# A hybrid decoder step whose free engines get their order from the scheduler's timeline model instead of its core model

## The chip, the cores and the metric

The kernel runs on one core of one Trainium2 chip. What is measured is the time of one execution on the device, in microseconds (us). TensorE (PE in the profile; PEld is its weight load), VectorE (DVE), ScalarE (ACT), GpSimd (POOL) and SyncE (SP, which here issues nearly all DMAs) each work through a queue of their own, strictly in the order in which it was written at build time. An instruction that waits holds up everything behind it on its engine. That order is what this change is about.

## The reference

Two layers of a decoder trunk, in float32, on 1024 prompt positions and on 8 x 4 sample positions that have 8192 earlier positions in a paged cache. Each layer computes

```
proj = x @ w_in                       # 1024 -> 46 blocks of 128 columns
SSD  : causal conv, SiLU, chunked state-space scan (16 heads), gated RMSNorm
MLA  : latent attention (8 heads), prompt: causal; sample: over the cache pages
GDN  : causal conv, SiLU, chunked gated delta rule (4 heads x 128), gated RMSNorm
x    = layer_norm(alpha * x + concat(SSD, MLA, GDN) @ w_out)
```

and also returns the new latents, rotated keys, convolution tails and final states of both groups.

## The kernel before

All 1056 positions (1024 of the prompt, 32 of the samples) go through together, in three column blocks of 384, 384 and 288. Activations stand transposed, channels on the partitions. A product that has to be near float32 is made of three matmuls of split operands (`mm3`, lines 182 to 186): `split` (line 161) has ScalarE copy the high part and GpSimd or VectorE subtract for the low part.

Each layer has two phases.

`phase1` (line 518) runs three things at once: the input projection as a filler, and two streams of recurrences, a and b (delta rule heads, latents, state-space pairs). The projection (`proj_block`, line 369) makes 24 matmuls for one of 46 x 3 blocks into one of two PSUM buffers of the tag `pj`; the block is then taken out of PSUM by `conv` (line 448; ScalarE copies at lines 464, 470 and 471), `gate` (line 496; a ScalarE tanh and a VectorE product that reads PSUM, both by the helpers at lines 156 and 159) or a plain copy at line 510. `conv` goes on with VectorE multiply-adds, a ScalarE tanh and a store to DRAM, from where the recurrences load it again. The recurrences (`gdn_block`, line 700, `ssd_pair`) are chains of small products on TensorE, each followed by a VectorE, ScalarE or GpSimd step. The method `merge` (line 397) writes down TensorE's order: it picks the stream whose due time has come by its own count of TensorE time, and the filler otherwise.

`phase2` (line 1402) runs the attention over the cache (`decode_units`, line 1654) with the causal attention of the prompt woven in (`weave_decode`, line 431), and then the output projection (`out_proj`, line 1856; PSUM tag `m`), the rest of the prompt's attention woven into its start (`weave`, line 422), and the layer norm.

What sets the order of each queue:

- Inside `merge` TensorE's order is the order of the program text, as `merge` interleaved it, and inside `weave_decode` that holds for TensorE and VectorE (`manual_schedule`, lines 410 and 435).
- Everywhere else the order is found when the kernel is built: the framework's scheduler runs the program on a model of the machine and fills each queue as it goes. An instruction can be placed when the model says that what it needs is there; of several that can, the one that is earlier in the program text goes first, or one from a `high_priority` block (the copies out of PSUM at lines 463, 469 and 501, the weight loads at line 365 and a few more). So ScalarE's, GpSimd's and SyncE's whole queues, VectorE's outside the decode, and all of them in the output projection are the scheduler's.
- The semaphores follow from that order. A queue keeps it on the chip whether or not the chip's times agree with the model's.

The tiles, their buffer counts and the due times in the `yield` statements are part of the source.

## Time and profile before

| | |
|---|---|
| median of three runs | 3574.2 us (3568.78 to 3581.75) |
| profiled execution | 3572.76 us, span 3571.0 us |
| TensorE busy | 3124.5 us, 87% |
| VectorE busy | 2234.9 us, 63% |
| ScalarE busy | 1337.2 us, 37% |
| GpSimd busy | 1124.5 us, 31% |
| mean granted TensorE clock | 0.939 |

Busy is the time in which an engine executes; a queue that stands at a wait isn't busy. Where the profile says "idle before" or "waited for", it names who ended the idle time. The layers repeat: the first takes the span's first half, the second the other. In each, the projection with the recurrences lasts some 1050 us, the decode some 500, the output projection some 300.

### The profile page before, as it was taken

The numbers are of one execution on the slowest core, as the hardware profiler recorded it, in microseconds if no ns is written. First come the engines' busy times: TensorE is split into PE (matmuls) and PEld (weight loads), VectorE is DVE, ScalarE is ACT, GpSimd is POOL, SyncE is SP. The second block draws the span as 40 slices with busy tenths as digits, with TensorE's granted clock in tenths as the row PEclk, the third lists the DMA queues.
The fourth block names the chain that finished last, engine by engine and source line by source line (L and its number), as shares of the span: only waits on it lengthen the run. The fifth ranks groups of instructions, "written<-read, shape, count | busy, mean of one in ns | idle before, by whom it ended". The sixth has DMA issues, their size and how long they took to land. (4 is left out here: it accounts for less than half of the span.)

```text
span 3571.0 us, 82553 instructions
## 1 busy us (share of the span) xinstructions
PE 3124.5 (87%) x33880; PEld 2666.9 (75%) x33880; DVE 2234.9 (63%) x4646; ACT 1337.2 (37%) x3099; POOL 1124.5 (31%) x1214
## 2 busy tenths in 40 slices
PE   6889999888778988979979999898987788889797
PEld 5888988888665655559878899887886566556697
DVE  7766365687545766745586653657865466666455
ACT  5433234333133344434434332343322343434344
POOL 4434344644421211101134444355453111211000
PEclk7999999999888999989989999999998799999898
DMA  3322324555776655444424232255567755553453
GB/s 137 123 90 88 106 67 161 168 169 177 249 251 201 207 178 191 171 154 157 151 83 126 83 94 90 68 171 184 173 214 254 230 191 190 183 196 128 161 180 127
DMA packets 317070, 564.70 MB, mean 158 GB/s; under 512 B 51772, under 2 KB 218748, under 8 KB 299668
## 3 DMA queue, kind: packets, MB, share of 16 engines
q1 hardware_dynamic: 293140, 408.42, 35.9%
q0 software_dynamic: 23552, 151.01, 12.0%
q8 instruction: 266, 4.36, 0.5%
q14 instruction: 112, 0.92, 0.1%
HBM read 429.00 MB, written 130.30 MB: 157 GB/s over the span
## 5 line engine op out<-in xcount | busy, mean ns | idle before, releaser
L180 PE MATMUL ps_pj<-xh,w_r 128*128 128x384 f32 (+1 forms) x4416 | 1212.7, 342 | 50.8 <-ACT p_cv L471 17.2
L180 PEld LDWEIGHTS ps_pj<-xh,w_r 128*128 128x128 f32 x4416 | 816.1, 196 | 71.0 <-ACT p_cv L471 19.1
L180 PE MATMUL ps_pj<-xl,w_r 128*128 128x384 f32 (+1 forms) x2208 | 733.9, 332 | 4.6 <-POOL xl L153 4.0
L180 PEld LDWEIGHTS ps_pj<-xl,w_r 128*128 128x128 f32 x2208 | 432.4, 196 | 13.5 <-POOL xl L153 11.1
L180 PE MATMUL ps_m<-mix,wo 128*128 128x384 f32 (+1 forms) x2304 | 395.4, 333 | 44.1 <-DVE wo L153 19.3
L180 PEld LDWEIGHTS ps_m<-mix,wo 128*128 128x128 f32 x2304 | 385.4, 196 | 50.8 <-DVE wo L153 22.4
L156 DVE SCALAR_TENSOR_TENSOR p_cv<-p_cv,c 128x384 f32<-128x384 f32 (+1 forms) x432 | 335.0, 779 | 71.9 <-ACT p_cv L159 65.9
L180 PE MATMUL ps_dS<-dec_k,c 32*32 32x256 f32 x8192 | 314.7, 385 | 31.5 <-issue 12.8
L153 POOL TENSOR_TENSOR w_r<-w_raw,w_r 128x1024 fp32r<-128x1024 f32 (+1 forms) x98 | 233.2, 2379 | 293.5 <-ACT w_r L165 251.3
L180 PEld LDWEIGHTS ps_dS<-dec_k,c 32*32 32x32 f32 x8192 | 190.1, 106 | 135.7 <-issue 85.0
L1667 DVE STREAM_TRANSPOSE dec_k<-dec_v 128x2048 f32<-128x2048 f32 x128 | 290.9, 2282 | 0.1
L1643 POOL DMA_INDIRECT dec<-cache_k_rope,c x64 | 60.9, 951 | 566.0 <-DVE dec L1736 516.9
L153 DVE TENSOR_TENSOR wo<-c,wo 128x1024 fp32r<-128x1024 f32 x96 | 119.0, 1243 | 128.2 <-PE ps_m L180 98.3
L159 ACT ACTIVATE p_cv<-p_cv 128x384 f32<-128x384 f32 x144 | 72.8, 505 | 314.8 <-DVE p_cv L156 313.8
L1470 ACT COPY c<-ps_aT 128x512 f32<-128x512 f32 (+3 forms) x192 | 89.9, 478 | 248.0 <-PE ps_aT L150 241.2
L165 ACT CAST wo<-c 128x1024 fp32r<-128x1024 f32 x96 | 100.4, 1050 | 218.3 <-DMA c<-w_out 174.9
L1643 POOL DMA_INDIRECT dec_v<-cache_kv_latent,c x128 | 120.8, 943 | 182.9 <-PE ps_dV L180 157.6
L180 PE MATMUL ps_b<-p_b 128*128 128x128 f32 (+7 forms) x1476 | 156.8, 284 | 21.1 <-ACT p_b L1024 8.4
L1513 DVE TENSOR_REDUCE c<-ps_aS 128x1 f32<-128x512 f32 (+3 forms) x192 | 105.4, 549 | 101.7 <-PE ps_aS L180 96.3
L159 ACT ACTIVATE c<-ps_aS,c 128x512 f32<-128x512 f32 (+3 forms) x192 | 110.6, 576 | 153.7 <-DVE c L1514 138.6
L318 POOL TENSOR_TENSOR c<-c,c 128x3 f32<-128x3 f32 (+2 forms) x22 | 17.1, 783 | 472.6 <-DVE c L317 472.6
L180 PEld LDWEIGHTS ps_b<-p_b 128*128 128x128 f32 (+5 forms) x1476 | 133.6, 161 | 37.7 <-ACT p_b L1024 9.9
(325 smaller groups left out, 5601.6 us busy)
## 6 DMA issues: line engine op xcount, KB each, us to landing
c<-w_out SPq DMA_DIRECT2D x96, 512.0 KB
w_raw<-w_in SPq DMA_DIRECT2D x92, 512.0 KB
pd<-p_cv SPq DMA_DIRECT2D x164, 192.0 KB
p_b<-pd SPq DMA_DIRECT2D x66, 256.0 KB
c<-pd SPq DMA_DIRECT2D x64, 256.0 KB
q<-rowd SPq DMA_DIRECT2D x48, 256.0 KB
p_b<-rowd SPq DMA_DIRECT2D x48, 256.0 KB
pd<-p_cv SPq DMA_DIRECT2D x82, 144.0 KB
```

Of the source, the lines that this page charges most:

```text
L153: eng.tensor_tensor(out=out, in0=a, in1=b, op=op)
L156: self.nc.vector.scalar_tensor_tensor(out=out, in0=a, scalar=s, in1=b, op0=op0, op1=op1)
L159: self.nc.scalar.activation(out=out, in_=in_, func=func, **kw)
L165: self.nc.scalar.copy(out=hi, in_=src)
L180: return self.nc.tensor.matmul(out, lhsT=lhsT, rhs=rhs, start=start, stop=stop)
L318: nc.gpsimd.tensor_tensor(out=r[:p, u], in0=r[:p, u], in1=self.mhalf[:p, 0:1].to_broadcast([p, u.stop - u.start]), op=ALU.pow)
L1470: nc.scalar.copy(out=t[:, :w], in_=p[:, :w])
L1513: nc.vector.reduce_max(out=m, in_=ps[:, :w], axis=AX.X)
L1643: nc.gpsimd.indirect_dma_start(out=out, out_offset=None, in_=src, in_offset=bass.IndirectOffsetOnAxis(ap=idx[:, c:c + 1], axis=0))
L1667: nc.vector.transpose(T[r].rearrange("p j s k -> p j (s k)"), V[:, :, r * 128:r * 128 + 128])
```

## The change

One argument of the context in which the kernel is built. The source of the kernel itself, its tiles, its instructions and the orders written out by hand stay as they are; the scheduler runs the program on another model of the machine (the timeline model, with its own times for instructions, transfers and the clock of TensorE) and fills the free queues by that one.

```
     outs = {k: nc.dram_tensor(k, s, F32, kind="ExternalOutput").ap() for k, s in OUTS.items()}
-    with tile.TileContext(nc) as tc:
+    with tile.TileContext(nc, schedule_with_timeline_sim=True) as tc:
         Builder(tc, ins, outs).build()
```

## Rows read from the trace of the kernel before

**Rows 1.** The page's head: span, then busy us and share by engine.
```profile
span 3571.0 us, 82553 instructions
...
PE 3124.5 (87%) x33880; PEld 2666.9 (75%) x33880; DVE 2234.9 (63%) x4646; ACT 1337.2 (37%) x3099; POOL 1124.5 (31%) x1214
```

**Rows 2.** Busy by stretch: start:end, length, engines (instructions), TensorE clock, DMA share, GB/s.
```profile
100.00:900.00 800.00, 727.05 (x6802) 686.06 (x6801) 514.65 (x1072) 286.27 (x704) 363.48 (x402) 0.96 0.41 128
1900.00:2700.00 800.00, 729.67 (x6871) 687.17 (x6869) 507.49 (x1073) 280.80 (x695) 379.88 (x413) 0.97 0.43 136
1100.00:1500.00 400.00, 355.89 (x6733) 233.86 (x6731) 269.67 (x602) 164.12 (x429) 76.60 (x82) 0.99 0.56 190
2900.00:3300.00 400.00, 362.61 (x6833) 236.96 (x6832) 274.42 (x612) 166.16 (x428) 72.63 (x77) 0.98 0.52 178
```

**Rows 3.** The same in 100 us steps: TensorE's least and most busy, projection and decode.
```profile
100.00:200.00 100.00, 85.43 (x700) 81.08 (x699) 72.39 (x132) 37.02 (x89) 33.80 (x45) 0.93 0.38 124
...
1200.00:1300.00 100.00, 88.18 (x1660) 57.06 (x1655) 68.17 (x158) 39.87 (x114) 19.82 (x21) 0.97 0.56 191
...
2100.00:2200.00 100.00, 98.71 (x1172) 93.43 (x1172) 40.07 (x101) 28.48 (x86) 37.29 (x35) 1.00 0.33 103
...
3200.00:3300.00 100.00, 93.38 (x1764) 60.36 (x1762) 69.33 (x153) 43.70 (x106) 13.19 (x14) 0.98 0.41 140
```

**Rows 4.** TensorE's waits by who ended them: us in total, times, longest us.
```profile
PE ps_pj L180 <- DMA cq<-cqd: 19.2, 4, 9.2
PE ps_a L180 <- ACT c L1024: 18.7, 2, 9.5
PE ps_a L180 <- DVE c L153: 18.4, 2, 9.5
...
PE ps_m L180 <- ACT mix L165: 17.9, 2, 9.9
PE ps_pj L180 <- ACT p_cv L471: 17.2, 6, 4.0
...
PE ps_pj L180 <- DVE p_cv L156: 13.9, 10, 4.9
...
PE ps_pj L180 <- ACT p_cv L464: 1.6, 2, 0.9
...
PE ps_b L150 <- DMA p_b<-pd: 2.5, 2, 1.6
```

**Rows 5.** TensorE in order of time around 664 us: start, length, instruction, [idle <-ended by].
```profile
664.13 0.27 PE L150 MATMUL ps_a<-c,c 128*128 128x128 f32 x1
673.57 0.79 PE L180 MATMUL ps_a<-c 128*128 128x128 f32 x2 [9.17 <-ACT c L1024]
674.16 0.42 PE L150 MATMUL ps_a<-c,c 128*128 128x128 f32 x1
```

**Rows 6.** ScalarE in the same stretch.
```profile
669.42 0.63 ACT L159 ACTIVATE q<-q 128x512 f32<-128x512 f32 x1 [8.41 <-DVE q L1092]
669.95 0.46 ACT L464 COPY p_cv<-ps_pj 128x384 f32<-128x384 f32 x1
...
672.95 0.57 ACT L1024 COPY c<-ps_a 128x512 f32<-128x512 f32 x1
```

**Rows 7.** VectorE in the same stretch.
```profile
665.09 6.47 DVE L1092 TENSOR_SCALAR q<-q,c 128x128 f32<-128x128 f32 x7 [4.16 <-DMA q<-rowd]
```

**Rows 8.** Busy by stretch behind that stall.
```profile
674.00:678.00 4.00, 3.96 (x22) 3.40 (x22) 3.37 (x6) 2.02 (x7) 2.43 (x2) 0.67 0.17 41
678.00:682.00 4.00, 4.00 (x29) 3.92 (x28) 3.94 (x5) 1.94 (x4) 3.13 (x3) 1.00 0.20 74
```

**Rows 9.** VectorE by line and shape: count, busy us, mean ns, idle before and its enders.
```profile
L1092 DVE TENSOR_SCALAR q<-q,c 128x128 f32<-128x128 f32 x128 | 44.9, 411 | 23.7 <-DMA q<-rowd 19.4 <-POOL p_b L153 4.3
```

**Rows 10.** ScalarE's longest wait in total, over the whole run.
```profile
ACT p_cv L159 <- DVE p_cv L156: 314.7, 120, 7.9
```

**Rows 11.** SyncE's queue: what its DMA issues waited for.
```profile
SPq L136 <- DVE p_cv L156: 422.2, 148, 11.0
```

## The prediction

> **What bounds the kernel now.** I read the page's head first, then the busy time by stretch, then what TensorE waited for, then the queues around one long wait. The chain of waits names TensorE most, but its listing covers only the last fifth of the run, so I go by stretches.
>
> TensorE is busy 3124.5 of 3571.0 us [rows 1]; the next engine stands at 63%. So the time is TensorE's work plus 446.5 us in which it waits. The change touches no instruction, and in the projection stage and in the decode TensorE's own order is written out by hand. What can move is the 446.5 us, and the clock with it. I split it by stage:
>
> - Projection with recurrences, 1600 us of it in two stretches: 800 - 727.05 and 800 - 729.67, together 143.3 us idle [rows 2].
> - Decode, 800 us: 44.1 + 37.4 = 81.5 us idle [rows 2].
> - The rest (start, ends of the projections, output projections): 446.5 - 143.3 - 81.5 = 221.7 us.
>
> Two things show that the free queues have a say in this. First, in front of one stall of 9.17 us [rows 5] the copy that TensorE needs (line 1024) stood in ScalarE's queue behind an exponential that waited 8.41 us for VectorE, as did a copy out of a projection buffer at line 464 [rows 6]; VectorE in turn had stood 4.16 us at a DMA and then took 6.47 us for seven small operations [rows 7]. The scheduler had placed the exponential first because its model had it ready by then, and on the chip it wasn't. The total for that copy is 18.7 us in two waits, the longer 9.5 [rows 4]: once in each layer. Second, ScalarE stood 314.7 us in 120 waits at a tanh of the convolution that VectorE hadn't fed yet [rows 10]. Most of that costs nothing, as ScalarE is idle 63% of the time.
>
> **The change part by part.** It adds, removes and lengthens no instruction; it permutes the free queues. No row shows the new order, so each part is bounded from both sides by rows of the old one.
>
> (1) Copies out of the two projection buffers. There are 2 x 46 x 3 = 276 blocks, and TensorE waited for the copy behind one in 6 + 10 + 2 = 18 of them, 17.2 + 13.9 + 1.6 = 32.7 us, so 1.8 us each [rows 4]. All of it can go: -33 us. On the other side 258 blocks are covered today; if one in five of these (52) came to wait 1.8 us, +94 us. That is the asymmetry on which my sign rests: a permutation can win back only the places that stall now, and has many more to lose. I take half as many again, nine blocks: +16 us.
>
> (2) The pair of stalls at line 1024. Between -18.7 (both go) and +18.7 (a like pair arises elsewhere; both layers have the same program, so a bad place comes twice). I take even odds that it goes and nothing like it arises: -9 us.
>
> (3) The other recurrence steps. Of the 143.3 us, 143.3 - 32.7 - 18.7 = 92 us are left for them (a little more, since part of the 32.7 lies outside). Each is a small VectorE, ScalarE or GpSimd step between two products. I take a sixth more, +15 us, by the argument of (1).
>
> Parts (1) to (3) have a common bound from the rows: sixteen stretches of 100 us, the best with 98.71 busy, the worst with 85.43 [rows 3]. All like the best: 16 x 1.29 = 20.6 us idle, -123. All like the worst: 16 x 14.57 = 233.1, +90. My sum for the three, +22, lies nearer to today's middle than to either end, because the order by text and priority remains the rule in both models.
>
> (4) Decode. TensorE and VectorE are fixed here, and only ScalarE, GpSimd and SyncE can be permuted, with TensorE and VectorE as cover. Eight stretches, best 93.38, worst 88.18 [rows 3]: between 53.0 us idle (-28) and 94.6 (+13). I take 0.
>
> (5) The rest. Its long waits are six of about 9 us: 19.2 on the load of the latents (two of its four waits are the long ones), 18.4 on an addition in front of the absorbed queries, 17.9 on the first split of the mixed rows [rows 4]. Together 55.5 us, so -55 to +55. These follow from stores and loads that must come one after the other, so I don't see them go; I take even odds for one more pair of 9 us, +9 us. Here TensorE's order in the output projection is free as well, but a product there still can't pass its weights.
>
> (6) The clock. Behind the 9.17 us stall the granted clock was 0.67 for 4 us, then 1.00 [rows 8], and a transpose took 0.42 us where the one before the stall took 0.27 [rows 5]: the level of 1.2 GHz, after an idle engine. That loses 4 x 0.33 = 1.3 us, 14% of the stall. I put 14% on the net.
>
> Sum: 16 - 9 + 15 + 0 + 9 = +31, with the 14% +35. The profiled execution took 3572.76 us (1.8 us around its span; 1.4 under the median of the runs), so 3608 us.
>
> The seven operations of [rows 7] took 0.92 us each, where the mean of their group is 0.41 [rows 9]: the duration depends on what runs beside. A plan made from one duration for each instruction misses such places under either model, so I take 0.05 off the chance of a gain and give it to my forecast. The Trainium skill, page "SBUF — State Buffer", section "Who interferes with whom", says why such a thing can be: a VectorE instruction with two SBUF inputs, or in a two-port mode, and a GpSimd instruction that reads SBUF block one another for a whole instruction, and the order of issue decides who stands. It speaks against any gain from a better plan; at 0.92 for 0.41 us on all 128 of that group VectorE would have 65 us more to do, of which the part on TensorE's path is shown by no run so far.
>
> **The rivals.**
>
> Faster: the timeline model's readiness comes nearer to the chip's. For it: the misplaced exponential, and the 120 waits of ScalarE at the tanh [rows 6, 10], are errors of the present model. Against it: little of them reaches TensorE. If the pair of (2) goes and a third of (1), 18.7 + 11 = 30 us, with the clock 34: 3539 us.
>
> No change: the order differs where there is slack, or hardly differs, since text order and priority remain; the change then does not do what it says. For it: TensorE is fixed over most of the run and busy 91% in the projection stage. Against it: thousands of instructions are free to move, and one misplaced instruction cost 18.7 us. 3573 us.
>
> Slower by SyncE's queue: a load that a recurrence needs comes to stand behind a store whose VectorE step is late. SyncE waited 422.2 us in 148 places for the convolution's last step, the longest 11.0 us [rows 11], and TensorE hardly ever for a load of the recurrences (2.5 us in all for the recurrences of stream b) [rows 4], so the loads now go out early enough. It decides once the added wait is longer than the lead that the source gives such a load, 7.85 us by the `yield` in `gdn_head`. With 16 half heads and 32 state-space blocks there are 48 groups of loads; if a quarter, 12, came late by half the longest wait, 5.5 us: +66 on my forecast without its parts (1) and (3), 3572.8 + 66 = 3639, with the clock 3648 us.
>
> **How the numbers follow.** Forecast (3585 to 3640 as its own range) 0.38; SyncE's queue 0.10; faster 0.32; no change 0.20. A measurement of this kernel can tell about 0.3%, 11 us, from no change. So faster 0.32, same 0.20, slower 0.48. The range takes in the faster case down to a full win of (1) and most of (2), 3572.8 - 47 = 3525, and goes up to the SyncE case and a little beyond, 3672; the extremes of the bounds (-123 and +90 in the projection stage alone) I leave out with 2 in 10.
>
> **What would show it.** Right: TensorE busy unchanged at about 3125 us or a little more, idle up by some 30; the waits on `ps_pj` up from 32.7 us in 18 places, spread over more blocks; decode's idle within 10 us of 81.5. Part (2) shows by whether a wait of about 9 us on line 1024 is still there. SyncE's rival would show as TensorE, or VectorE ahead of it, waiting for `pd` and `rowd` loads. I am wrong if the waits on `ps_pj` fall and the idle sum with them, or if the decode moves by tens of us although TensorE and VectorE stand as before, or if the output projection, where all orders are free, makes most of the difference.

## The result and the profile after

The changed kernel took 3525.1 us (median of 4 runs, 3518.9 to 3534.9) where the kernel before took 3571.5 beside it: ratio 0.9871, interval 0.9836 to 0.9907, so 1.3% faster. I had forecast 3608 us and a slower kernel; the time lies at the lower edge of the range, next to its case of a gain. On another chip the same pair gave 0.9854 (0.9840 to 0.9869). The profiled execution took 3522.7 us against 3572.8: 50.1 us less.

The page's head of the kernel after:

```profile
span 3520.9 us, 82628 instructions
...
PE 3101.4 (88%) x33880; PEld 2651.4 (75%) x33880; DVE 2235.5 (63%) x4646; ACT 1329.9 (38%) x3099; POOL 1137.2 (32%) x1214
```

TensorE's idle time fell from 446.5 to 3520.9 - 3101.4 = 419.5 us, and its busy time by 23.1 us although its products are the same. Part of that is the clock: it lost (1 - 0.939) x 3571.0 = 218 us before and, at a mean of 0.943, 201 after, an estimate of some 17 us from the two means. That is a third of the gain; the other 6 us of busy time no run explains.

The four stretches of [rows 2], cut in the trace of after at the same matmuls:

```profile
114.90:901.70 786.80, 723.78 (x6800) 685.68 (x6800) 507.29 (x1059) 284.23 (x703) 371.30 (x404) 0.97 0.42 130
1878.70:2677.70 799.00, 731.97 (x6870) 689.02 (x6868) 508.44 (x1072) 279.79 (x696) 385.71 (x411) 0.96 0.44 137
1089.30:1490.80 401.50, 356.56 (x6734) 235.12 (x6736) 269.23 (x602) 163.51 (x429) 76.72 (x82) 0.99 0.56 190
2857.70:3258.60 400.90, 358.73 (x6833) 234.05 (x6831) 274.12 (x613) 165.18 (x428) 72.64 (x77) 0.99 0.52 178
```

In the projection stage TensorE stood 63.0 + 67.0 = 130.0 us (143.3 before), in the decode 44.9 + 42.2 = 87.1 (81.5 before). What lies outside of these stretches lost 19.3 us of idle and 18.9 us of busy time: 38 of the 50 us.

TensorE's order is the same in both kernels but for the output projection, so the start of one matmul can be compared in both traces. Between such points (the first and last products of a stage, and a few within):

```
stretch, us in the trace of before      change, us
start of layer 1, 0 to 100                 +14.7
projection of layer 1, to 1025             -10.4
its end and the absorb, to 1075            -11.9
decode of layer 1, to 1579                  +1.5
output projection of layer 1, to 1800      -18.7
start of layer 2, to 1900                   +3.4
projection of layer 2, to 2775              -7.1
its end and the absorb, to 2832            -11.2
decode of layer 2, to 3338                  -1.6
output projection of layer 2, to 3550       -9.9
end                                         +1.1
sum                                        -50.1
```

The gain stands in four short places: the two output projections (-28.6) and the two joins in front of the decode (-23.1). The projections' -17.5 and the starts' +18.1 cancel, and in the first layer they are largely the same thing: of the 14.7 us that the start loses, 1.7 are left by 500 us. Each row is one execution against one. A second pair of traces (e4 and e5 below, each on a chip of its own) has the gain in the same places: output projections -16.5 and -7.3, joins -10.5 and -10.2.

The waits that answer to [rows 4], in the trace of after:

```profile
...
PE ps_m L180 <- ACT mix L165: 19.9, 2, 11.9
PE ps_pj L180 <- DVE p_cv L156: 19.7, 12, 4.7
PE ps_b L180 <- DVE p_b L153: 19.0, 7, 9.3
PE ps_a L180 <- DVE c L153: 17.5, 2, 8.8
PE ps_pj L180 <- DMA cq<-cqd: 15.3, 4, 5.1
...
PE ps_pj L180 <- ACT p_cv L464: 7.4, 4, 3.6
PE ps_b L150 <- DMA p_b<-pd: 7.1, 4, 2.2
...
PE ps_pj L180 <- ACT p_cv L471: 6.7, 6, 3.1
```

The line "DVE c L153" has almost its old total, but it is another wait. Before, it was the absorb's addition, 8.9 and 9.5 us; that wait is gone. What bears the name now is the stall that stood under "ACT c L1024": the same matmul in the middle of the projection, in front of which TensorE now waits for VectorE:

```profile
672.43 0.80 PE L180 MATMUL ps_a<-c 128*128 128x128 f32 x2 [8.76 <-DVE c L153]
```

The output projection, first and last product of each layer: first the kernel before, then after (columns as in [rows 2]). It lasts 221 and 212 us before, less than the 300 that I gave above.

```profile
1579.00:1800.00 221.00, 204.54 (x1180) 199.69 (x1179) 123.63 (x185) 92.81 (x141) 22.90 (x21) 0.93 0.48 164
3337.80:3550.20 212.40, 199.91 (x1180) 196.21 (x1180) 120.10 (x185) 86.04 (x125) 1.73 (x2) 0.95 0.50 172
```

```profile
1572.60:1775.30 202.70, 194.96 (x1180) 191.73 (x1180) 122.76 (x185) 92.16 (x141) 24.72 (x21) 0.97 0.53 176
3296.50:3499.00 202.50, 194.93 (x1179) 191.77 (x1180) 119.56 (x185) 85.38 (x125) 1.74 (x2) 0.97 0.54 180
```

The same products: 28.2 us less in all, of it 13.6 idle and 14.6 busy, at a granted clock of 0.97 for 0.93 and 0.95. Here the clock accounts for all of the busy time: it lost 15.5 + 10.6 = 26 us before and 6.1 + 6.1 = 12 after. What TensorE waited for there, by the second operand, in before and then in after:

```profile
PE ps_m L180 <- DVE wo L153: 19.3, 10, 4.6
```

```profile
PE ps_m L180 <- ACT wo L165: 12.4, 9, 3.4
...
PE ps_m L180 <- DVE wo L153: 2.8, 4, 1.4
```

The weight's low half (VectorE's subtraction) came late ten times before, because layer-norm work stood ahead of it in VectorE's queue. The longest of these waits, before 1745.69 us, in the kernel before: ScalarE had made the high half by 1737.1, and VectorE came to the low half at 1744.4.

```profile
1736.01 1.05 ACT L165 CAST wo<-c 128x1024 fp32r<-128x1024 f32 x1 [1.90 <-DMA c<-w_out]
```

```profile
1737.80 2.41 DVE L156 SCALAR_TENSOR_TENSOR c<-ps_aT,c 128x384 f32<-128x384 f32 x5
...
1744.42 1.22 DVE L153 TENSOR_TENSOR wo<-c,wo 128x1024 fp32r<-128x1024 f32 x1
```

In front of the decode it is SyncE's queue. Before (start, length, issue):

```profile
1025.06 8.34 SPq L136 DMA_DIRECT2D q<-qd  x14
1033.45 0.51 SPq L136 DMA_DIRECT2D c<-w_ukT  x1
1033.99 2.60 SPq L136 DMA_DIRECT2D c<-qd  x4
```

and after:

```profile
947.10 0.48 SPq L136 DMA_DIRECT2D c<-w_ukT  x1
...
994.60 0.64 SPq L136 DMA_DIRECT2D c<-qd  x1
...
998.42 1.39 SPq L136 DMA_DIRECT2D q<-qd  x3
...
1028.10 1.28 SPq L136 DMA_DIRECT2D c<-qd  x2
...
1035.36 1.71 SPq L136 DMA_DIRECT2D c<-qxr  x4
```

Before, the absorb's loads (w_ukT and four of qd) stood behind the prompt's fourteen query loads, all in one lump after the last store of qd. After, they are strewn between the stores, as each becomes possible: w_ukT goes out 86 us earlier, and two of the absorb's four loads of qd and nine of the fourteen query loads go out ahead of the last store. The wait before ended with the addition, which needs the loads of qd and not w_ukT; so what counts is the last of these loads. From the last store of qd to the addition it took 17.3 us before and 8.7 after.

### The profile page after: what moved, and what is told of

Same layout as the page of the kernel before. It is cut to its first block, busy times and chain, and to the rows that moved or that the text cites. A ratio compares the mean times of both kernels' runs of the same rounds, so it can differ in the third digit from the quotient of the medians.

```text
span 3520.9 us, 82628 instructions
## 1 busy us (share of the span) xinstructions
PE 3101.4 (88%) x33880; PEld 2651.4 (75%) x33880; DVE 2235.5 (63%) x4646; ACT 1329.9 (38%) x3099; POOL 1137.2 (32%) x1214
## 5 line engine op out<-in xcount | busy, mean ns | idle before, releaser
L180 PE MATMUL ps_pj<-xh,w_r 128*128 128x384 f32 (+1 forms) x4416 | 1219.2, 343 | 57.6 <-DVE p_cv L156 19.7
L180 PE MATMUL ps_m<-mix,wo 128*128 128x384 f32 (+1 forms) x2304 | 386.4, 328 | 35.2 <-ACT mix L165 19.9
L180 PEld LDWEIGHTS ps_m<-mix,wo 128*128 128x128 f32 x2304 | 377.0, 192 | 41.8 <-ACT mix L165 20.1
L156 DVE SCALAR_TENSOR_TENSOR p_cv<-p_cv,c 128x384 f32<-128x384 f32 (+1 forms) x432 | 357.0, 828 | 77.1 <-ACT p_cv L159 69.1
L180 PE MATMUL ps_dS<-dec_k,c 32*32 32x256 f32 x8192 | 315.1, 383 | 14.6 <-DVE dec_k L1667 5.8
L153 POOL TENSOR_TENSOR w_r<-w_raw,w_r 128x1024 fp32r<-128x1024 f32 (+1 forms) x98 | 234.2, 2389 | 286.6 <-ACT w_r L165 191.9
L153 DVE TENSOR_TENSOR wo<-c,wo 128x1024 fp32r<-128x1024 f32 x96 | 119.1, 1242 | 121.9 <-PE ps_m L180 92.0
L165 ACT CAST w_r<-w_raw 128x1024 fp32r<-128x1024 f32 (+1 forms) x98 | 100.2, 1023 | 151.6 <-PE ps_pj L180 136.2
```

What stands on the lines that cost most here:

```text
L153: eng.tensor_tensor(out=out, in0=a, in1=b, op=op)
L156: self.nc.vector.scalar_tensor_tensor(out=out, in0=a, scalar=s, in1=b, op0=op0, op1=op1)
L165: self.nc.scalar.copy(out=hi, in_=src)
L180: return self.nc.tensor.matmul(out, lhsT=lhsT, rhs=rhs, start=start, stop=stop)
```

## The experiments

Each ratio is against the kernel before, run beside it on the same chip: it took 3501 to 3504 us on three of the chips used and 3574 to 3577 on two others, so times are compared by ratio. "Core" means that the kernel is ordered by the core model, as before.

```
                                     ratio (interval)         us
e5   after, again                    0.9854 (0.9840-0.9869)  -51
e1   core, weight splits first       0.9921 (0.9900-0.9941)  -28
e2   core, absorb first in the text  1.0030 (1.0016-1.0044)  +10
e3   e1 and e2                       0.9961 (0.9945-0.9977)  -14
e6   core, absorb and queries first  1.0021 (1.0008-1.0034)   +7
e7   e6 and e1                       0.9961 (0.9946-0.9976)  -14
e9   e6, gated first as well         0.9992 (0.9979-1.0005)   -3
e10  e9 and e1                       0.9931 (0.9915-0.9947)  -24
e13  core, absorb loads by ScalarE   1.0010 (0.9998-1.0022)   +4
e14  e13 and e1                      0.9943 (0.9924-0.9961)  -20
e17  e13, gated first as well        0.9994 (0.9977-1.0011)   -2
e18  e17 and e1                      0.9907 (0.9886-0.9929)  -33
e11  core, block for the scheduler   1.0029 (1.0016-1.0042)  +10
e12  that block, timeline model      0.9976 (0.9959-0.9994)   -8
e4   core, GpSimd in pieces          1.0001 (0.9986-1.0016)    0
e8   after, VectorE held at start    0.9851 (0.9839-0.9864)  -52
e15  after, second chunk apart       0.9888 (0.9872-0.9905)  -40
e16  e15, weight splits, ScalarE     0.9876 (0.9857-0.9895)  -44
```

**The output projection.** In the core-model kernel the weight splits go under high priority:

```diff
+                with self.tc.high_priority():
+                    w = self.split(None, raw, None, next(Rw), next(Rw), self.nc.vector)
+                yield w
-                yield self.split(None, raw, None, next(Rw), next(Rw), self.nc.vector)
```

> The kernel before (core model) with one edit: in the output projection the split of each weight half (ScalarE copy and VectorE subtraction) stands under high priority. In the trace of before TensorE waited 19.3 us in 10 places for that subtraction (DVE wo L153), in the trace of after 2.8 in 4, and the output projections run some 30 us shorter there (21 in the first layer, 9 in the second). Theory A (two places: the weight splits stood behind layer-norm work in VectorE's queue, and the absorb loads behind the query loads in SyncE's): the waits for DVE wo fall under 5 us, the two output projections get 15 to 30 us shorter with the clock, the time falls to about 3548 us (-0.4 to -0.8%). Theory B (TensorE's own freed order, and the better order all over, made the gain, not this place): the waits move to ScalarE's copies or to the layer norm, the output projections stay within 6 us, the time within 0.2% of before.

-28 us, theory A, at the top of what it gave. The waits of e1:

```profile
PE ps_m L180 <- ACT wo L165: 5.6, 3, 3.1
...
PE ps_m L180 <- DVE wo L153: 2.6, 4, 0.7
```

The two output projections took 201.8 and 202.9 us from first to last product; with before's order on the same chip (e4) they took 217.0 and 209.7, with after's on another chip (e5) 200.5 and 202.4. So one priority gives what the timeline model gave there. It also moves TensorE's own order a little: at 96 of its 33880 places another product stands than before (112 in after), all in the output projection. How much of the gain is that no run separates; the waits on wo fell from 16.8 us (e4) to 2.6.

The counter-test lets the timeline model order that part alone, beside a control with the same block and the core model:

```diff
-                for nb in range(3):
+                with self.tc.block(name="op", schedule_with_timeline_sim=True):
+                  for nb in range(3):
```

> Control for the next one: the kernel before with the loop over the three token blocks of the output projection put into a block of its own for the scheduler, which keeps the core model there too. The queues differ from before only at the ends of that block. Expected by both theories: 0 to +10 us, since nothing can be moved across its ends.

> The same kernel with the timeline model for that block alone; all else is ordered by the core model. Theory A: the output projections carry about half of the net gain, -20 to -30 us against the control beside it, and TensorE's waits for DVE wo fall from 17 us to under 5. Theory B (the gain there needs the order of the stages ahead, or is spread): under -8 us.

The block costs 10 us. Within it the timeline model gains 0.9976 / 1.0029 = 0.9947, so 19 us, give or take some 8 by the two intervals; theory A had 20 to 30, theory B under 8. The waits for DVE wo fell from 16.2 to 7.9 us, less than A had said; the output projections from 212.7 and 206.8 us to 199.2 and 199.1.

**In front of the decode.** Five attempts to take away the 9 us by hand, under the core model. The first swaps two steps of the text:

```diff
-                next(self.mla)
                 absorb = self.absorb()
                 next(absorb)
+                next(self.mla)
```

> The kernel before with one edit: in phase1 the absorbed queries are started ahead of the prompt's first query loads, so five loads stand ahead of twelve on SyncE's queue; no other queue changes. TensorE waited 8.9 us (first layer) and 9.5 us (second) for the addition fed by these loads; in after no such wait is left, and the load of w_ukT starts 86 us earlier. Theory A: nearly the whole wait goes in both layers, with the clock that it costs 10 to 12 us a layer, so -18 to -24 us, about 3550 us. Theory B (the load's own way to landing and the later join set the time, the wait only moves to the scores of the prompt, whose query loads are now 3 us later): under -6 us in all.

> Both edits together, still under the core model. Theory A: they add up, -35 to -50 us, so 3522 to 3537 us, level with after (3525): the timeline model's gain is these two places, and what it wins and loses elsewhere cancels (start +20, projections -17). Theory B (gain spread over many places): not more than -12 us, so over 3559.

Slower than either theory had it (the query loads that now stand behind are fourteen, not twelve), and e3 shows that the two edits add up (-28 + 10 = -18, measured -14). The absorb's wait fell to 5.1 us, but VectorE then stood for a piece of gated:

```profile
1086.82 0.29 DVE L156 SCALAR_TENSOR_TENSOR c<-ps_aO,c 128x128 f32<-128x128 f32 x1 [14.75 <-DMA c<-gated]
```

The second leaves the text and puts the three steps under high priority:

```diff
+                with self.tc.high_priority():
-                next(self.mla)
-                absorb = self.absorb()
-                next(absorb)
+                    next(self.mla)
+                    absorb = self.absorb()
+                    next(absorb)
```

> The kernel before (core model) with the absorb loads and the prompt's first query loads, and the steps behind them, under high priority; text order unchanged. In SyncE's queue the load of w_ukT and the loads of qd then stand between the stores of qd and no longer in one block behind them, as in after. Moving the absorb loads ahead in the text alone cost 10 us: the wait of 8.9 us fell to 5.1, but the query loads, then at the end of a block of 19, made TensorE wait 14.2 us at a copy (line 1530). Theory A (the place is SyncE's block of loads, all of it; after wins its 26 us there by spreading them): both waits go, -18 to -26 us, about 3480 where before takes 3503. Theory B (the last store of qd sets the time, whatever stands behind it): within 6 us of before.

> The edit of the weight splits (-28 us alone) and the edit of the absorb and query loads together, under the core model. Theory A: -46 to -54 us, ratio 0.985 to 0.987, level with the changed kernel beside it, so that these two places are the whole net gain of the timeline model and the rest cancels. Theory B: clearly behind the changed kernel, by 15 us or more.

> The changed kernel again, beside the kernels below. The other experiments ran on a chip on which the kernel before takes 3503 us, 2% less than on the first one, with most of the difference in the decode. Both theories expect the ratio found first, 0.987, so some 3457 us where before takes 3503.

Theory A fell. The absorb's wait is gone in e6, and the load of w_ukT and those of qd stand between the stores, but:

```profile
1078.86 0.29 DVE L156 SCALAR_TENSOR_TENSOR c<-ps_aO,c 128x128 f32<-128x128 f32 x1 [17.50 <-DMA c<-gated]
```

The third takes that load, in `values`, forward too:

```diff
-                    self.dma(gt, self.gated[:, pr, i * 128:i * 128 + 128])
+                    with self.tc.high_priority():
+                        self.dma(gt, self.gated[:, pr, i * 128:i * 128 + 128])
```

> As the run with the absorb and query loads under high priority (+8 us), with one load more under high priority: the 128x128 piece of gated that each pair of heads needs. In that run the wait of 9.6 us before the absorb was gone, but VectorE then stood 17.5 us for such a piece, issued at 1075 us where before has it at 1048, behind seven query loads and three of the decode. Theory A (SyncE's order at the end of the projection is the place; after has these loads all early): with this load early as well both waits are gone in both layers, -15 to -26 us against before. Theory B (each load taken forward puts another one late on the same queue): a further wait of 5 us or more turns up between 1050 and 1130 us, and the time stays within 8 us of before.

> That kernel and the weight splits under high priority (-28 us alone). Theory A: -43 to -54 us, level with the changed kernel (-51 us on this chip): the net gain is the output projections and SyncE's order in front of the decode. Theory B: -15 to -30 us, no more than the weight splits alone.

Theory B. Both waits are gone, and TensorE's waits between 1025 and 1125 us now are

```profile
PE ps_aT L150 <- ACT c L1532: 7.2, 8, 2.0
PE ps_dS L180 <- DMA c<-qxr: 6.6, 2, 6.2
PE ps_pj L180 <- DMA ck<-ckd: 3.0, 1, 3.0
```

a load of the decode's queries and one of the latents. The fourth issues the absorb's five loads from ScalarE's queue:

```diff
-        self.dma(wkt[0:64], self.i["w_ukT"][l])
+        self.dma(wkt[0:64], self.i["w_ukT"][l], nc.scalar)
...
```

> The kernel before (core model) with the absorb's five loads issued from ScalarE's queue in place of SyncE's; TensorE's and GpSimd's orders are the same as before, SyncE has five loads less in its block. Theory A (SyncE's queue in front of the decode is full, so that any load taken forward there puts another one late; off that queue nothing gets late): the wait of 9 us before the absorb goes in both layers and nothing takes its place, -16 to -26 us. Theory B (the joining of the stores and loads takes this long in any case): the wait stays over 5 us, or ScalarE, standing at a load that waits for a store, delays its copies of kT; within 8 us of before.

> That kernel with the weight splits of the output projection under high priority as well (-28 us alone). Theory A: -44 to -54 us, level with the changed kernel (-51 us on this chip) under the core model, so that these two places are its net gain. Theory B: -20 to -30 us.

The wait before the absorb fell from 8.9 to 2.8 us, so theory A is right on that place and B on the time; again it was gated: VectorE stood 12.25 us for such a piece at 1081.96 us.

The fifth joins the fourth and the third's priority for gated:

> The kernel before (core model) with the absorb's five loads on ScalarE's queue and the pieces of gated under high priority on SyncE's. Theory A (the 22 us in front of the decode are SyncE's order alone): the waits for both are gone, nothing takes their place, -16 to -24 us against before. Theory B (the place can't be mended load by load; another load of that block, of the decode's queries or the next prompt queries, gets late): within 8 us of before, with a new wait of 4 us or more between 1050 and 1130 us.

> The same with the weight splits of the output projection under high priority. Theory A: -40 to -52 us, level with the changed kernel (ratio 0.985 to 0.987), both places together making up its net gain. Theory B: -20 to -32 us, the weight splits alone.

Theory B once more; the wait now is for the decode's queries (1000 to 1125 us of e17):

```profile
PE ps_dS L180 <- DMA c<-qxr: 7.8, 2, 6.8
```

because the loads of qxr went out late, behind others of the same queue:

```profile
1058.72 0.56 SPq L136 DMA_DIRECT2D dec_k<-gated  x1
...
1060.51 0.38 SPq L136 DMA_DIRECT2D c<-qxr  x1
...
1070.40 0.34 SPq L136 DMA_DIRECT2D c<-gated  x1
1070.78 0.43 SPq L136 DMA_DIRECT2D c<-qxr  x1
...
1074.55 0.31 SPq L136 DMA_DIRECT2D c<-qxr  x1
```

What held SyncE's queue up from 1045 to 1080 us of e17:

```profile
SPq L136 <- PE ps_aS L180: 11.0, 1, 11.0
SPq L136 <- DVE c L1529: 8.4, 2, 5.1
```

The first is the wait ahead of the decode's own load of gated (1058.72), the other two are waits ahead of pieces of gated that the edit had taken forward: such a load stands at the head of the queue until TensorE or VectorE releases it, and the loads of qxr stood behind it. In after all four are out by 1037 us. Each attempt removed or shortened the wait that it named, and another of 6 to 18 us took its place, on TensorE or on VectorE. What after has is an order of the whole queue in which none of these loads is late. That this is SyncE's queue alone, and not also the other engines' orders, no run shows, nor that a better order by hand can't be had: each of the five moved whole groups of loads. With the weight splits these kernels came to -14 (e7), -24 (e10), -20 (e14) and -33 us (e18), all at theory B or within 2 us of it. The best, e18, has 0.9907, where after has 0.9854 on one chip and 0.9871 on another; no chip ran the two side by side.

**The stall in the middle of the projection** (part 2 of the prediction), which stands in both kernels. GpSimd's four products of 128x1024 in `gdn_sample` were cut into quarters:

```diff
-            self.tt(nc.gpsimd, S[:, h], S[:, h], ...)
+            for z in range(0, 8, 2):
+                self.tt(nc.gpsimd, S[:, h, z:z + 2], S[:, h, z:z + 2], ...)
```

> The kernel before with GpSimd's four products of 128x1024 in gdn_sample (state times decay, 1.9 us each) cut into four pieces of 128x256 each; VectorE's order stays. At the stall of 9.2 us (9.5 in the second layer) seven VectorE operations of line 1092 took 6.47 us beside these products, and in the trace of after the same matmul, the 5693rd, stands again 8.8 us with four of them in 5.83 us. Theory: VectorE stands for a whole GpSimd instruction, so neither model's order can remove the stall; with pieces the seven take 3 us or less, and the stall falls to about 6 us, so -3 to -4 us a layer, under what can be told of the time. Rival: their length comes from something else (the DMAs beside them), and it stays over 5.5 us with the stall at 9.

The stall is 10.6 us, not 6, so the forecast fell. But VectorE's order did not stay: an operation of line 978, which stood behind seven of these operations before, stands behind two in e4, and there it waited for a step of GpSimd. VectorE in e4:

```profile
671.93 0.35 DVE L978 TENSOR_SCALAR p_b<-ps_b,p_b 128x128 f32<-128x128 f32 x1 [2.58 <-POOL p_b L674]
672.20 1.71 DVE L1093 TENSOR_SCALAR q<-q,c 128x128 f32<-128x128 f32 x6
```

So the eight operations themselves got shorter, 3.06 (the two ahead of line 978) + 1.71 = 4.8 us for 6.8, and the wait for GpSimd took the place of what was won. On what the theory says of the two engines, operations taken one at a time tell more than merged rows. The first of the eight on VectorE, with GpSimd (POOL) beside it, before and then in e4:

```profile
665.09 2.00 DVE L1092 TENSOR_SCALAR q<-q,c 128x128 f32<-128x128 f32 x1 [4.16 <-DMA q<-rowd]
665.11 1.89 POOL L153 TENSOR_TENSOR p_b<-p_b,c 128x1024 f32<-128x1024 f32 x1
```

```profile
666.30 2.49 DVE L1093 TENSOR_SCALAR q<-q,c 128x128 f32<-128x128 f32 x1 [3.96 <-DMA q<-rowd]
666.38 2.33 POOL L153 TENSOR_TENSOR p_b<-p_b,c 128x256 f32<-128x256 f32 x4
```

Of the first seven before, three took 1.92 to 2.00 us, and each ended 0.1 us behind a product of GpSimd; the other four took 0.27 to 0.28. In e4 the first ended 0.1 us behind the fourth quarter in a row; three more took 0.36 to 0.65, each ending 0.1 us behind one quarter; the last four, with no quarter beside them, took 0.27 each. So an operation of VectorE here did stand until an instruction of GpSimd had ended. The Trainium skill, page "SBUF — State Buffer", section "Who interferes with whom", has whichever of the two issues first hold the pair of ports that they share for its whole instruction, with the other blocked. The 2.00 us beside 1.89 agree with the blocking; that one operation stood for four instructions in a row, the rule as I read it doesn't say, and it remains open.

**The start of the changed kernel, and whether its order is luck.** e8 holds VectorE's order in the first layer norms as the text has it (under a condition, left out here, that picks them):

```diff
-        with soon():
+        with soon(), self.tc.manual_schedule(engines={mybir.EngineType.DVE}):
             for c in range(8):
```

e15 gives the second weight chunk a place of its own:

```diff
-        raw = self.Rraw(1024)
+        raw = self.Cv.a[:, 1568:2592] if c == 1 else self.Rraw(1024)
```

e16 adds the weight splits of e1 and the loads of e13 to e15.

> The changed kernel with one edit: VectorE's order in the first half of the first layer norms is held as written, so that each centring is followed by its addition again; the timeline model had put eight centrings first and TensorE waited 9.3 us there (5.8 before). The first 100 us of after run 14.7 us longer than before's. Theory: the first block gets its 3.4 us back and the blocks behind it part of the rest, -5 to -12 us against the changed kernel beside it. Rival: the loss comes from SyncE's order (w_raw loads behind x) and ScalarE's, and under 3 us come back.

> The changed kernel with one edit: the second weight chunk of each layer is loaded into a part of the convolution's ring, so its load needn't wait until the first chunk is split. In after that load starts at 10.0 us behind eleven loads of x (before: 7.8 us, behind six), lands at 17.4, and GpSimd splits it beside the first layer norm's additions, one of which took 2.38 us where the others took 0.55. Theory A (this order is what makes the start slow): the wait of 9.3 us before the layer norm's sum falls by 3 us or more and the first 100 us get 3 to 12 us shorter, so -3 to -12 us against the changed kernel. Theory B (VectorE's and ScalarE's order, spread over the first 100 us): within 3 us of it.

> The changed kernel with the second weight chunk apart, the weight splits under high priority and the absorb loads on ScalarE's queue. If what helped under the core model was the same thing that the timeline model already found, the last two add nothing here: some 2 to 6 us for waits on wo that are left (14 us in 16 places), and the start's -3 to -12 us, so 3435 to 3450 where before takes 3502 (ratio 0.981 to 0.985). If they were other gains, down to 3400 us.

None is clearly better than the changed kernel; e16, expected at 0.981 to 0.985, has 0.9876. In e8 the wait before the first layer norm's sum became 10.0 us (9.1 in e5): the text's order, held strictly, makes VectorE wait for each square. In e15 it fell from 9.3 to 7.3 us, but the products behind it stood between 1.2 us ahead of those of after and 2.9 us behind them. So the start's loss is neither of the two alone, and its cause stays open. It also costs little: in after, e5, e8, e15 and e16 alike the 15 to 18 us by which they lie behind before's order at 100 us are 0 to 3 by 500 us. By 1200 us the trace of e15 lay 19 us behind that of after, that of e16 with the same edit 1.5 us. Whether such differences are the order or the execution these single traces don't tell. The side of these runs that I use: each gave the timeline model a somewhat different kernel to order, and it stayed 40 to 52 us ahead of before. A gain that was one lucky permutation would hardly do that. How much of any one result is luck stays open: e15 and e16 ran on another chip than e5 and e8, without after beside them.

## Why the prediction was wrong

**The sign.** It rested on "a permutation can win back only the places that stall now, and has many more to lose". The count of places was right and the inference wrong: the many covered places stayed covered (part 1, below); why, no run shows. Idle time in the projection stage fell by 13 us where parts (1) to (3) had it rise by 22. That the time still falls on the lower edge of the range, 3525, is chance: the edge was drawn for a full win of part (1) and most of part (2), and neither moved.

**Part (5) is the step that failed**: "These follow from stores and loads that must come one after the other, so I don't see them go" and "a product there still can't pass its weights". I gave it +9 us; the joins and output projections made -51.7, the two starts +18. Of the six long waits that it names, the pair in front of the absorbed queries went (18.4 us to none), the pair on the load of the latents fell from 9.1 and 9.2 to 5.1 and 4.8 us, and the pair on the mixed rows stayed (17.9, now 19.9). The absorb's wait was only in part the length of a chain of stores and loads: half of the 17.3 us from the last store to the addition was a place in SyncE's queue, behind fourteen query loads. That it stood there is shown by the traces; that moving it alone would win it is not, as five attempts failed. And a product that can't pass its weights does come earlier if the weights do; the waits for wo, 19.3 us in ten places, have no term in the prediction, though they are as long as the longest that it names. The prediction named this as what would make it wrong: the output projection made more than half.

**Part (1)**: +16 forecast; 19.7 + 7.4 + 6.7 = 33.8 us in 22 places against 32.7 in 18, so +1.

**Part (2)**: -9 forecast, half of a gain and a like pair. The stall stayed at the same matmul, 8.8 and 8.7 us, under another releaser's name. That one plan from fixed durations misses such a place under either model was right; two other places, of 5.8 (p_b L153) and 5.3 us (p_sa L153) before, grew to 9.3 and 8.0.

**Part (3)**: +15 forecast. All of the projection stage together changed by -13.3 idle.

**Part (4)**: 0 forecast; +1.5 and -1.6 us in the two decodes. Right, with idle up by 5.6 within 10.

**Part (6)**: 14% on the net forecast. Measured 23.1 us of busy time on 27.0 of idle, 86%, or 63% if only the 17 us that the mean clock explains are counted. My price came from one 9.17 us stall [rows 8], and that was the wrong stall to take it from: most of the half clock lay inside the stall itself, where there was nothing to lose: (1 - 0.62) x 10 = 3.8 us of it in the row below, against the 1.3 us behind the stall that I counted.

```profile
664.00:674.00 10.00, 0.83 (x6) 0.59 (x5) 8.64 (x13) 3.29 (x6) 8.13 (x8) 0.62 0.49 150
```

In the output projection shorter stalls cost about as much of the clock as they last (below).

**SyncE's queue as a rival**: its sign was wrong and its place too. Waits for the loads of the recurrences rose only from 2.5 to 7.1 us (`p_b<-pd`); where the queue decided, it gained.

## What to carry to other kernels

Before putting a price on a better scheduler, list the waits whose releaser was itself waiting only in a queue: a load of an input that goes out late, a split that has its data. Those can go, however long they have been there. And judge an order of a DMA queue as a whole: five times a late load was put first, and five times another wait took its place, in e17 in part because a load put first wasn't ready and held up the queue.

## What the runs showed of the hardware

A stall of 4.57 us in the output projection of before was followed by 8 us at half clock, though work was at hand:

```profile
1745.69 2.29 PE L180 MATMUL ps_m<-mix,wo 128*128 128x288 f32 x8 [4.57 <-DVE wo L153]
```

```profile
1746.00:1750.00 4.00, 4.00 (x18) 3.81 (x18) 1.87 (x4) 1.05 (x1) 0.67 (x1) 0.50 0.70 258
1750.00:1754.00 4.00, 3.73 (x16) 3.38 (x16) 1.13 (x3) 0.54 (x1) 1.13 (x2) 0.50 0.01 4
1754.00:1758.00 4.00, 4.00 (x28) 4.00 (x27) 4.00 (x7) 4.00 (x9) 2.73 (x3) 0.84 0.00 0
```

At 0.50 (1.2 GHz) for 8 us and 0.84 for 4 it lost 4.0 + 0.6 = 4.6 us, as much as the stall. Over both output projections of before the rows above give 26 us lost to the clock on 29 us of idle, and 12 on 15 in after. So short stalls weighed nearly double in this stage of dense products.

Chips differ in one stage: with before's order the decode from 1100 us on had 6733 products in 400 us on the first chip [rows 2] and as many in 370 on another (e4), at no higher clock (0.97 for 0.99), while the projections agreed within some 5 us; the cause is open:

```profile
1100.00:1470.00 370.00, 332.37 (x6761) 220.51 (x6760) 270.40 (x598) 161.52 (x425) 78.70 (x84) 0.97 0.61 207
```
